# One encoder layer on one core: every product of x in Strassen blocks, the mixers in a stage of their own

## The chip, the cores and the metric

One core of a Trainium2 chip runs the whole layer. Its engines work side by side, each through its own queue in order: TensorE (PE, matrix products; its weight loads are listed as PEld), VectorE (DVE), ScalarE (ACT), GpSimd (POOL) and the DMA queues that SyncE (SP) issues. The metric is the device time of one execution in microseconds (us).

## The reference, cut to what matters

One layer with SEQ = 1024 rows and D_MODEL = 1024. x is multiplied by w_in (46 column tiles of 128) and by four gate matrices (32 column tiles). Four mixers of width 512 take parts of the first product.

```python
h = x @ w_in[l]
h_a, h_b, h_c, h_d = jnp.split(h, IN_SPLITS, axis=-1)
y_a = rglru_branch(...)        # convolution, two 64-wide gates, linear recurrence (scan), gelu
y_b = b_g * causal_dwconv(c_g * xh, sconv_w)
y_c = rwkv7_branch(h_c, ...)   # delta-rule recurrence over 1024 steps, 8 heads
y_d = chunk_attention(q, k, v, rel_bias)
merged = sum(sigmoid(x @ w_gate[n] + b_gate[n]) * (y[n] @ w_branch[n]) for n in range(4))
x = layer_norm(ALPHA * x + merged @ w_out, ...)
ff = square(relu(x @ w_ff1)) @ w_ff2
ple = (p @ w_ple) * sigmoid(x @ w_ple_gate + b_ple_gate)
x = layer_norm(ALPHA * x + ff + ple, ...)
```

## The kernel before, in words

Everything is kept transposed: a tile has 128 channels on the partitions and the 1024 rows along the free axis, in two halves of 512. A float32 product is made of three fast products: each operand is split into a high part (a copy by ACT, `Gemm.split` L347) and a low part (source minus high, by DVE, L348), and `Gemm.acc` (L367 to L369) adds high·high, high·low and low·high in a PSUM bank. With a depth of 1024, one column tile is 8 depth steps x 2 halves x 3 = 48 matmuls of 128x512.

The order of the program is as follows, with the times of the profile:

- 0 to 31 us: x comes in by eight 512 KB loads, and two column tiles (the low-rank inputs, C tiles 12 and 13) are accumulated in four banks as each slice of x lands.
- to about 115 us: six more C tiles (`zc_tile`) and `low_rank`, which makes decay, learning rate and gate of the RWKV mixer.
- about 115 to 977 us: the RWKV mixer, 16 units (two halves of the heads, eight stretches of 128 rows each). A unit inverts a triangular matrix in six levels; one level is a small product (`py` L246), an add on DVE (L247), a transpose on PE (`pt` L231) and a copy out on ACT (L232), each waiting for the one before. A unit runs at a raised priority (`HP`), and other work is put beside it: `run(oth, NO)` emits NO = 5 half column tiles of 24 matmuls (NOB = 6 in the first four units), held back by `issue_after` to behind the last inverse product of an earlier unit (L259, the unit's mark). That other work is the rest of the C tiles, q, k and v, then the recurrence `lru(j)` (L571 to L625) and the short convolution `sconv(j)` (L628 to L645) for j = 0 to 3, both reading their products straight from PSUM, and a few gate tiles.
- about 977 to 1040 us: three gate tiles, and loads of the finished branch outputs.
- 1040 to 1490 us: chunk attention, eight heads in 64 steps (`attend`), beside the branch products (`br`) and the remaining gate tiles (`ggt`).
- 1490 to 2413 us: w_out, layer norm, the seven-product feed-forward one (`seven`, L1054 on: a pair of weight tiles times x, as 2 x 2 blocks, takes 7 block products instead of 8, with sums of weight blocks on POOL and x blocks made on POOL and DVE beforehand), then feed-forward two and the last layer norm.

x stays split in 16 buffers throughout. A scheduler fixes the order of each engine's queue before the run; on the chip each queue is followed strictly in order, and an instruction at the head that waits holds what stands behind it.

Of the kernel before, what the change touches and what calls it, by code (L numbers as in the profile page):

```python
# [45 lines left out]
class Rwkv:  # L46
# [7 lines left out]
    PTAG = {"pt": "r", "py": "r", "p12": "r", "po": "o", "px": "s", "pss": "s", "pp": "s", "py2": "s"}  # L54
    BUFS = {t: 2 for t in ("ar", "bk", "bkT", "AA", "Qs", "TTf", "W", "SV", "bv", "D", "zt", "gn", "wm")}
    BUFS["gg"] = 3
    ALT = ("YT", "Y", "Yo")
# [30 lines left out]
    def unit(s, hf, b):  # L88
# [5 lines left out]
        def ps(n, w=512):  # L94
            tag = s.PTAG.get(n, "q")
            if tag == "r":
                tag += str(b % 2)
            return s.psum.tile([128, w], F32, tag=tag, name=n + u, bufs=PB[tag])

        def st(n, shape, tag=None, dt=F32):  # L100
            tag = tag or n
            if tag in s.ALT:
                tag += str(b % 2)
            return s.pool.tile(shape, dt, tag="rw_" + tag, name=n + u, bufs=s.BUFS.get(tag, 1))
# [150 lines left out]
        R = st("R", [128, 4, 128], dt=F32R)  # L255
# [9 lines left out]
        for c in range(2):  # L265
# [3 lines left out]
            PD = st("PD", [128, 2, 128])  # L269
# [51 lines left out]
HP = 3000  # L321
LAG = 2
NO = 5
NZ = 10
NB = 3
SK = 0
LO = 2
L0 = 3
N0 = 4
NOB = 6  # L330
DP = 2
PF = 4
NG = 14
NH = 8
NA = 1.6
# [37 lines left out]
def trunk(ctx, tc, xT, xn, pT, w_in, w_gate, w_branch, w_out, w_ff1, w_ff2, w_ple, w_pg,  # L373
# [6 lines left out]
    psum = ctx.enter_context(tc.tile_pool(name="psum", bufs=2, space=PSUM))  # L380
    bp = ctx.enter_context(tc.tile_pool(name="bp", bufs=1))
    tp = ctx.enter_context(tc.tile_pool(name="tp", bufs=4))
# [4 lines left out]

    def ps(tag, name, w=512):
        return psum.tile([128, w], F32, tag=tag, name=name, bufs=PB[tag])
# [3 lines left out]
    qkv = dr.tile([3, 4, 128, 1024], F32, name="qkv")  # L393
    gsd = dr.tile([32, 128, 1024], F32, name="gsd")
# [3 lines left out]
    xs = []  # L398

    def gemm_x(w, name, tag="g"):  # L400

        w = gm.load(w, 1024, name)
        for h in range(2):
            p = ps(tag, f"g{name}{h}")
            sl = slice(h * 512, h * 512 + 512)
            gm.acc(p, [w[k] + (xs[k][0][:, sl], xs[k][1][:, sl]) for k in range(8)])
            yield h, sl, p

    def gate(g):

        for h, sl, p in gemm_x(w_gate[g // 8, g % 8], f"gt{g}"):
            t = tmp(f"tg{g}{h}")
            A.activation(t, p, AF.Tanh, scale=0.5, bias=hbg[:, g:g + 1])  # L413
            yield h, sl, t

    def spill(g):
        for h, sl, t in gate(g):
            SY.dma_start(gsd[g, :, sl], t)
            yield 1

    spilled = [g for g in range(16) if g % 8 >= 1 + g // 8 * SK][:NG]


    with tc.tile_pool(name="mx", bufs=1) as mx:
        def t4(name, w=1024):
            return mx.tile([128, w], F32, tag="t4", name=name, bufs=6, padded_shape=[128, 1028])
# [7 lines left out]
        wt = [wp.tile([128, 1024], F32, tag="wf", name=f"wfc{i}", bufs=2) for i in (12, 13)]  # L434
        wf0 = [[], []]

        def first(i, c):
            wf, kw = wt[i][:, c:c + 512], [dict(name=f"w{t}c{12 + i}{c}") for t in "hl"]
            SY.dma_start(wf, w_in[W_C + 12 + i][:, c:c + 512])
            if i and c:  # L440
                wh, wl = (mx.tile([128, 512], F32R, tag=f"rw_{t}0", **k) for t, k in zip(("YT", "Y"), kw))
            else:
                wh, wl = (wp.tile([128, 512], F32R, tag=t, **k) for t, k in zip(("wh", "wl"), kw))
            gm.split(wf, wh, wl)
            wf0[i] += [(wh[:, k:k + 128], wl[:, k:k + 128]) for k in range(0, 512, 128)]

        zp = [[ps(t, f"gc{12 + i}{h}") for h in range(2)] for i, t in enumerate("gq")]
        first(0, 0)
        for k in range(8):
            xf = t4(f"xf{k}")  # L450
            SY.dma_start(xf, xT[k])
            xh = bp.tile([128, 1024], F32R, tag=f"s1_{k}", name=f"xh{k}")
            xl = bp.tile([128, 1024], F32R, tag=f"s2_{k}", name=f"xl{k}")
            gm.split(xf, xh, xl)
            xs.append((xh, xl))
            for i, c in {0: [(1, 0)], 1: [(0, 512)], 2: [(1, 512)]}.get(k, []):
                first(i, c)
            for i in range(2):
                for h in range(2):
                    sl = slice(h * 512, h * 512 + 512)  # L460
                    gm.acc(zp[i][h], [wf0[i][k] + (xh[:, sl], xl[:, sl])], k == 0, k == 7)
# [5 lines left out]
        V.tensor_scalar(hbg, hbg, 0.5, None, op0=ALU.mult)  # L467
        nh = cp.tile([128, 4], F32, name="nh")
        G.memset(nh, -0.5)

        cst = mx.tile([128, C_N], F32, name="cst")
        SY.dma_start(cst, cstd[:, 128:])
        pv = mx.tile([128, len(PV), 4], F32, name="pv")
        SY.dma_start(pv, pvd)
        mu = mx.tile([128, 2, 14], F32, name="mu")
        SY.dma_start(mu[:, 0, :], mud)
# [9 lines left out]
        def shifted(x, n, sl):  # L486
            return x[:, sl.start + n:sl.stop + n]
# [20 lines left out]
        def low_rank(d):  # L508


            def rw(tag, name, dt=F32R):
                return mx.tile([128, 512], dt, tag="rw_" + tag, name=name, bufs=R.BUFS[tag])
# [754 lines left out]
```

## Time and profile before

| | us |
|---|---|
| median of 3 runs | 2414.67 (2410.48 to 2416.7) |
| profiled execution, its own time | 2414.82 |
| span of the profiled execution | 2413.0 |
| PE busy | 2369.2 (98%), 12114 instructions |
| DVE busy | 1353.1 (56%) |
| ACT busy | 845.9 (35%) |
| POOL busy | 345.2 (14%) |
| mean granted TensorE clock | 0.990 of full speed |

Matmuls are pipelined, so the listed duration of one (about 395 ns) is longer than the distance between the starts of two, and a PE that counts as busy may still be switching or waiting between short instructions. The chain of waits gives 91% of the span to PE, 3% each to DVE and DMA.

### The profile page before, as it was taken

How to read it: one execution, taken by the hardware profiler on the slowest of the kernel's cores; microseconds unless marked ns; L12 is line 12 of the kernel's file. 1: busy time of each engine (PE TensorE's matmuls, PEld its weight loads, DVE VectorE, ACT ScalarE, POOL GpSimd, SP SyncE). 2: the span in 40 equal slices, each digit the busy share in tenths (PEclk: the TensorE clock that was granted, in tenths of full speed). 3: DMA queues.
4: the chain of work that ended last, by engine and by line, in shares of the span. 5: the costliest groups of instructions: out<-in, count | busy, mean ns of one | idle time of the engine just before them, and what ended most of it. 6: DMA issues, size and time to landing. Idle time of an engine off the chain costs nothing.

```text
span 2413.0 us, 31988 instructions
## 1 busy us (share of the span) xinstructions
PE 2369.2 (98%) x12114; PEld 1951.1 (81%) x12114; DVE 1353.1 (56%) x2758; ACT 845.9 (35%) x1478; POOL 345.2 (14%) x310
## 2 busy tenths in 40 slices
PE   9999999999999999999999999997999999999998
PEld 7888788777777778878888888876888888888886
DVE  5354545677677642245534334777644444776667
ACT  5543322424334222234434343334344444321110
POOL 0000100010000100000211100114145555000001
PEclk9999999999999999999999999998999999999999
DMA  5532222112121112254512224401123333532311
GB/s 200 192 126 70 88 71 70 56 53 66 53 71 53 64 60 77 98 174 125 158 53 73 80 76 142 164 31 57 44 96 111 112 114 130 187 123 89 103 53 70
DMA packets 123850, 231.33 MB, mean 96 GB/s; under 512 B 20016, under 2 KB 51888, under 8 KB 123696
## 3 DMA queue, kind: packets, MB, share of 16 engines
q1 hardware_dynamic: 123696, 229.29, 28.4%
q8 instruction: 95, 1.56, 0.3%
q14 instruction: 59, 0.48, 0.1%
HBM read 169.48 MB, written 59.77 MB: 95 GB/s over the span
## 4 chain that ended last, share of the span: by engine, by line
PE 91%; DVE 3%; DMA 3%; ACT 1%; issue 1%; POOL 0%; SPq 0%; DVEq 0%; ACTq 0%; POOLq 0%
PE f L368 5%; PE f L367 5%; PE f L369 5%; PE ggt L368 4%; PE ggt L369 4%; PE ggt L367 4%; PE af L369 2%; PE af L368 2%; PE af L367 2%; PE gc L368 2%; PE gc L369 2%; PE gc L367 2%; PE br L369 2%; PE br L367 2%; PE br L368 2%; PE gd L367 2%
## 5 line engine op out<-in xcount | busy, mean ns | idle before, releaser
L369 PE MATMUL ggt<-xh,wlgt 128*128 128x512 f32 x512 | 202.5, 396 | 0.0
L367 PE MATMUL ggt<-xh,whgt 128*128 128x512 f32 x512 | 202.4, 395 | 0.0
L368 PE MATMUL ggt<-xl,whgt 128*128 128x512 f32 x512 | 202.2, 395 | 0.0
L1183 DVE TENSOR_TENSOR x<-x,f 128x512 f32<-128x512 f32 x240 | 159.1, 684 | 74.1 <-PE f L369 73.4
L368 PE MATMUL f<-w2l,a2h 128*128 128x512 f32 x512 | 200.0, 391 | 0.0
L369 PE MATMUL f<-w2h,a2l 128*128 128x512 f32 x512 | 199.7, 390 | 0.0
L367 PE MATMUL f<-w2h,a2h 128*128 128x512 f32 x512 | 198.0, 390 | 0.0
L367 PEld LDWEIGHTS f<-w2h,a2h 128*128 128x128 f32 x512 | 96.0, 188 | 21.0 <-ACT w2h L347 0.3
L368 PEld LDWEIGHTS f<-w2l,a2h 128*128 128x128 f32 x512 | 96.1, 188 | 20.6
L369 PEld LDWEIGHTS f<-w2h,a2l 128*128 128x128 f32 x512 | 96.1, 188 | 20.6
L369 PEld LDWEIGHTS ggt<-xh,wlgt 128*128 128x128 f32 x512 | 96.2, 188 | 19.1 <-issue 0.5
L368 PEld LDWEIGHTS ggt<-xl,whgt 128*128 128x128 f32 x512 | 96.3, 188 | 19.0 <-issue 0.3
L367 PEld LDWEIGHTS ggt<-xh,whgt 128*128 128x128 f32 x512 | 96.3, 188 | 18.3
L367 PE MATMUL br<-yh,whwb 128*128 128x512 f32 x256 | 101.8, 398 | 3.2 <-ACT tg L413 1.8
L232 ACT ACTIVATE YT<-pt 128x512 fp32r<-128x512 f32 x96 | 56.8, 594 | 128.2 <-PE pt L231 126.0
L369 PE MATMUL br<-yh,wlwb 128*128 128x512 f32 x256 | 101.5, 396 | 0.1
L348 DVE TENSOR_TENSOR wlf<-wff,whf 128x512 fp32r<-128x512 f32 x80 | 65.7, 822 | 62.8 <-ACT whf L347 62.7
L368 PE MATMUL br<-yl,whwb 128*128 128x512 f32 x256 | 100.9, 394 | 0.0
L347 ACT ACTIVATE a2h<-a2f 128x1024 fp32r<-128x1024 f32 x32 | 34.0, 1061 | 177.9 <-PE f L368 109.4
L348 DVE TENSOR_TENSOR wlgt<-wfgt,whgt 128x512 fp32r<-128x512 f32 x64 | 46.8, 731 | 86.7 <-ACT whgt L347 84.5
L347 ACT ACTIVATE whf<-wff 128x512 fp32r<-128x512 f32 x80 | 50.6, 632 | 117.8 <-PE af L368 49.6
L369 PE MATMUL gc<-xh,wlc 128*128 128x512 f32 x224 | 88.1, 394 | 0.0
(490 smaller groups left out, 5962.6 us busy)
## 6 DMA issues: line engine op xcount, KB each, us to landing
wfgt<-w_gate SPq DMA_DIRECT2D x32, 512.0 KB, 3.3
wff<-w_ff SPq DMA_DIRECT2D x32, 512.0 KB, 3.3
a2f<-actd SPq DMA_DIRECT2D x32, 512.0 KB, 3.2
w2f<-w_ff SPq DMA_DIRECT2D x32, 512.0 KB, 3.9
gsd<-tg SPq DMA_DIRECT2D x44, 256.0 KB, 2.0
tl<-gsd SPq DMA_DIRECT2D x44, 256.0 KB, 3.1
zt<-zs SPq DMA_DIRECT2D x16, 640.0 KB, 4.9
qk<-qkv SPq DMA_DIRECT2D x64, 128.0 KB, 2.7
```

The lines of the kernel that those rows point to most:

```text
L232: A.activation(dst, heads(p), AF.Copy)
L347: s.nc.scalar.activation(hi, src, AF.Copy)
L348: s.nc.vector.tensor_tensor(lo, src, hi.bitcast(F32), op=ALU.subtract)
L367: mm(ps, lh, rh, start=first and i == 0, stop=False, **kw)
L368: mm(ps, lh, rl, start=False, stop=False, **kw)
L369: mm(ps, ll, rh, start=False, stop=last and i == n - 1, **kw)
L1183: V.tensor_tensor(x1[i][:, sl], x1[i][:, sl], p, op=ALU.add)
```

## The change

All 78 column tiles of x times w_in and w_gate are now made by `seven`, two tiles at a time: 39 pairs of 7 products, each product 4 depth steps x 3 = 12 matmuls. One pair takes 84 matmuls instead of 96. What else moves with it:

- x is kept as seven blocks (`XA`: 11, 21, T2, T1, T3, 22, T4, each split in four high and four low tiles), made at the start by `blocks()`: 4 subtractions on DVE, 12 on POOL, and 28 splits.
- Results come out in pieces at the end of several products. q, k, v go to DRAM unscaled (the 0.125 moves to the attention's loader), the 20 inputs of lru and sconv go to a new DRAM buffer `hd`, all 32 gates to `gsd`.
- To make room, RWKV's buffers are cut (single `YT`, `Y`, `Yo`, `AA`, `bk`, `TTf`; one PSUM bank `r0` for the inverse instead of two in turn). Beside a unit now stand NO = 11 products (NOB = 13 in the first four), 132 and 156 matmuls instead of 120 and 144.
- lru and sconv leave the RWKV stage. They run afterwards in a pool `my` of their own, with their inputs loaded from DRAM; sconv's two multiplications go to POOL. Four and eight of the remaining products stand between them in the program text.
- All gates are finished before the attention, x's pool is closed there, and the attention stands beside branch products only, in the order n = 2, 1, 0, with three steps (NA) per column tile.

```diff
-    PTAG = {"pt": "r", "py": "r", "p12": "r", "po": "o", "px": "s", "pss": "s", "pp": "s", "py2": "s"}
-    BUFS = {t: 2 for t in ("ar", "bk", "bkT", "AA", "Qs", "TTf", "W", "SV", "bv", "D", "zt", "gn", "wm")}
-    ALT = ("YT", "Y", "Yo")
+    PTAG = {"pt": "r0", "py": "r0", "p12": "r0", "po": "o", "px": "s", "pss": "s", "pp": "s", "py2": "s"}
+    BUFS = {t: 2 for t in ("ar", "bkT", "Qs", "W", "SV", "bv", "D", "gn", "gg")}
+    PB = {"r0": 1, "q": 2, "o": 1, "s": 1}
...
-NO = 5
-NOB = 6
-NA = 1.6
+NO = 11
+NOB = 13
+NA = 3
...
+    def seven(XB, w0, w1, name, done, tiles, bank, dst=None, load=None, sums=None):
...
+        a = bank("a", f"a{name}")
+        product(a11, 1, a, "11")
+        p1 = tiles(f"p1{name}")
+        A.activation(p1, a, AF.Copy)
+        yield 1
+        c = bank("c", f"c{name}")
+        product(a12, 2, c, "21")
+        result(0, 0, c, p1)
+        yield 1
+        s1 = total(1, a21, a22, ALU.add)
+        s2 = total(2, s1, a11, ALU.subtract)
+        product(s2, 3, a, "T2", first=False)
+        u2 = tiles(f"u2{name}")
+        A.activation(u2, a, AF.Copy)
...
+        product(s1, 4, b, "T1")
...
+        product(s3, 5, a, "T3", first=False)
...
+        product(s4, 6, b, "22", first=False)
...
+        product(a22, 7, a, "T4", first=False)
...
+        def blocks():
+            block("11", x11)
+            block("21", x21)
+            for k in range(4):
+                V.tensor_tensor(x11[k], x12[k], x11[k], op=ALU.subtract)
+            for k in range(4):
+                G.tensor_tensor(t2[k], x22[k], x11[k], op=ALU.subtract)
+            block("T2", t2)
+            block("T1", x11)
...
+        def others():
+            for i in (2, 6, 10):
+                yield from zc_pair(i)
+            for j in (0, 2):
+                for i in range(3):
+                    yield from qkv_pair(i, j)
+            for j in (0, 2):
+                for n in (0, 4, 12, 16, 8):
+                    yield from hd_pair(n + j)
+            for g in range(0, 32, 2):
+                yield from gate_pair(g)
...
-            for h, sl, p in gemm_x(w_in[W_A + j], f"xa{j}"):
-                A.activation(xa[:, 3 + h * 512:3 + h * 512 + 512], p, AF.Copy)
-                yield 1
+            SY.dma_start(xa[:, 3:1027], hd[j])
...
+            G.tensor_tensor(cx[:, 2:1026], cx[:, 2:1026], cc, op=ALU.mult)
...
-        oth = chain(zc(halves(1)), qkvs(), *(g for j in range(4) for g in (lru(j), sconv(j))), *(spill(g) for g in spilled[:NG - NB]))
+        for j in range(4):
+            sconv(j)
+            run(4)
+            lru(j)
+            run(8)
+        run(1000)
+    first.close()
...
-        for n in range(4):
+        attend(NA)
+        for n in (2, 1, 0, 3):
```

Three places in the queues follow, before and after. In the names, `lg` is a gate product of lru (the first digit after it is j), `gt` or `c` a product of a gate pair or C pair, `gya` a product of lru's second input; `py`, `pt`, `p12` with two numbers belong to the RWKV unit of that half and stretch.

The first is PE at the start. Before, the two first C tiles, 12 and 13, in four banks, where the second slice of x begins:

```order
L368 MATMUL gc130_101<-xl0_111,whc130_115 128x512
L368 MATMUL gc131_102<-xl0_111,whc130_115 128x512
L369 MATMUL gc130_101<-xh0_110,wlc130_116 128x512
L369 MATMUL gc131_102<-xh0_110,wlc130_116 128x512
L367 MATMUL gc120_99<-xh1_133,whc120_104 128x512
L367 MATMUL gc121_100<-xh1_133,whc120_104 128x512
L367 MATMUL gc130_101<-xh1_133,whc130_115 128x512
L367 MATMUL gc131_102<-xh1_133,whc130_115 128x512
```

Of the change, PE where the second product of pair c0 ends and the third product of pair c12 begins, and POOL's first sums up to the last part of the block T2 that this third product reads:

```order
L358 MATMUL cc0_276<-x21h3_245,whc02_277 128x512
L359 MATMUL cc0_276<-x21l3_246,whc02_277 128x512
L360 MATMUL cc0_276<-x21h3_245,wlc02_278 128x512
L358 MATMUL ac12_195<-xT2h0_314,whc123_334 128x512
L359 MATMUL ac12_195<-xT2l0_315,whc123_334 128x512
L360 MATMUL ac12_195<-xT2h0_314,wlc123_335 128x512
```

```order
L414 TENSOR_TENSOR S1c12_330<-wfA1_99 128x512
L414 TENSOR_TENSOR S2c12_332<-S1c12_330,wfA0_98 128x512
L443 TENSOR_TENSOR wfA1_99<-wfA0_98,wfA1_99 128x512
L533 TENSOR_TENSOR xT20_306<-xf220_128,xf000_101 128x512
L539 TENSOR_TENSOR xf010_120<-xf220_128,xf010_120 128x512
L533 TENSOR_TENSOR xT21_308<-xf221_130,xf001_103 128x512
L539 TENSOR_TENSOR xf011_122<-xf221_130,xf011_122 128x512
L533 TENSOR_TENSOR xT22_310<-xf222_132,xf002_105 128x512
L539 TENSOR_TENSOR xf012_124<-xf222_132,xf012_124 128x512
L543 TENSOR_TENSOR xf100_110<-xf100_110,xT20_306 128x512
L533 TENSOR_TENSOR xT23_312<-xf223_134,xf003_107 128x512
```

The first slice of x with two tiles of weights was all that PE needed for each step before; now its queue goes on to block T2, whose four parts are made by POOL behind and among other sums.

The second is PE at the end of RWKV unit 3 of the second half. Before:

```order
L596 MATMUL lg310_7047<-xc3_7030,wri3_6964 128x512
L231 MATMUL pt_1_3_6358<-ident_267,Y_1_3_6266 128x128 x4
L246 MATMUL py_1_4_6735<-Yo_1_4_6733,YT_1_4_6726 128x64 x4
L596 MATMUL lg311_7050<-xc3_7030,wri3_6964 128x512
L151 MATMUL pn_1_5_7126<-cst_274,sq_1_5_7124 128x2 x2
L231 MATMUL pt_1_4_6742<-ident_267,Y_1_4_6711 128x128 x4
L252 MATMUL py_1_3_6364<-idr_290 128x512
L254 MATMUL py_1_3_6364<-Y_1_3_6266,AA_1_3_6222 128x128 x4
L182 MATMUL pbg_1_5_7155<-rk_1_5_7152,cst_274 128x256
L259 MATMUL p12_1_3_6372<-YT_1_3_6357,R_1_3_6370 128x128 x4
L367 MATMUL gya31_7386<-xh0_110,whya30_7072 128x512
```

Of the change, the same unit:

```order
L360 MATMUL bgt4_7889<-xT1h3_386,wlgt44_7891 128x512
L227 MATMUL pt_1_3_7058<-ident_144,Y_1_3_6997 128x128 x4
L242 MATMUL py_1_3_7066<-Yo_1_3_7064,YT_1_3_7057 128x64 x4
L227 MATMUL pt_1_3_7073<-ident_144,Y_1_3_6997 128x128 x4
L242 MATMUL py_1_3_7082<-Yo_1_3_7079,YT_1_3_7072 128x64 x4
L227 MATMUL pt_1_3_7089<-ident_144,Y_1_3_6997 128x128 x4
L248 MATMUL py_1_3_7095<-idr_169 128x512
L250 MATMUL py_1_3_7095<-Y_1_3_6997,AA_1_3_6953 128x128 x4
L255 MATMUL p12_1_3_7103<-YT_1_3_7088,R_1_3_7101 128x128 x4
L358 MATMUL agt4_7828<-xT3h0_432,whgt45_8190 128x512
```

Before, the next unit's chain (unit 4 of the second half) and the lru products stand between the levels; now the levels follow one another with nothing between.

The third is PE at lru's products for j = 1. Before, in the middle of the RWKV stage:

```order
L246 MATMUL py_1_0_4846<-Yo_1_0_4844,YT_1_0_4835 128x64 x4
L219 MATMUL pw_1_0_4824<-SV_1_0_4818,AA_1_0_4793 64x64 x7
L596 MATMUL lg100_5167<-xc1_5156,wri1_5090 128x512
L246 MATMUL py_0_7_4474<-Yo_0_7_4471,YT_0_7_4464 128x64 x4
L231 MATMUL pt_1_0_4853<-ident_267,Y_1_0_4837 128x128 x4
L596 MATMUL lg101_5170<-xc1_5156,wri1_5090 128x512
L596 MATMUL lg110_5173<-xc1_5156,wri1_5090 128x512
L231 MATMUL pt_0_7_4481<-ident_267,Y_0_7_4389 128x128 x4
L246 MATMUL py_1_0_4861<-Yo_1_0_4859,YT_1_0_4852 128x64 x4
L596 MATMUL lg111_5176<-xc1_5156,wri1_5090 128x512
L151 MATMUL pn_1_1_5252<-cst_274,sq_1_1_5250 128x2 x2
```

Of the change, after the last product of the last gate pair, with all three last j's and then the attention's scores (`p20`):

```order
L359 MATMUL agt30_10873<-xT4l3_568,whgt307_10993 128x512
L360 MATMUL agt30_10873<-xT4h3_567,wlgt307_10994 128x512
L755 MATMUL lg100_9897<-xc1_9886,wri1_9881 128x512
L755 MATMUL lg101_9900<-xc1_9886,wri1_9881 128x512
L755 MATMUL lg110_9903<-xc1_9886,wri1_9881 128x512
L755 MATMUL lg111_9906<-xc1_9886,wri1_9881 128x512
...
L755 MATMUL lg211_10228<-xc2_10208,wri2_10203 128x512
L755 MATMUL lg300_10539<-xc3_10528,wri3_10523 128x512
...
L755 MATMUL lg311_10548<-xc3_10528,wri3_10523 128x512
L871 MATMUL p20_0_0_11082<-kh0_11037,q20_11036 128x128
```

On DVE the same stretch holds 17 instructions of j = 0 and then all of j = 1, 2, 3, with no split of a gate weight among them; before, the same 32 per j, and four multiplications, stand among those of RWKV units and weight splits.

## Rows read from the trace of the kernel before

**Rows 1.** The page: share of the chain of waits by engine.

```profile
PE 91%; DVE 3%; DMA 3%; ACT 1%; issue 1%; POOL 0%; SPq 0%; DVEq 0%; ACTq 0%; POOLq 0%
```

**Rows 2.** Busy time by stretch: start:end, length, PE, PEld, DVE, ACT, POOL (instructions), clock, DMA share, GB/s.

```profile
0.00:31.00 31.00, 28.45 (x116) 20.77 (x117) 20.73 (x55) 17.91 (x27) 1.91 (x15) 1.00 0.74 269
...
500.00:600.00 100.00, 98.59 (x588) 79.03 (x587) 72.00 (x164) 37.90 (x66) 10.03 (x15) 1.00 0.19 60
...
1750.00:2050.00 300.00, 300.00 (x1330) 248.38 (x1329) 137.16 (x169) 128.28 (x218) 158.07 (x121) 1.00 0.32 113
```

**Rows 3.** The chain of waits in order of time: start, length, what.

```profile
9.59 0.91 PE gc L367 x4
...
453.31 0.86 PE lg L596 x2
...
537.56 1.09 PE pq L195 x8
...
889.02 1.08 PE pq L195 x8
```

**Rows 4.** The timeline of DVE: two levels of one unit's inverse (start, length).

```profile
293.10 0.40 DVE L247 TENSOR_TENSOR Y<-Y,py 128x256 fp32r<-128x256 f32 x1
...
295.88 0.41 DVE L247 TENSOR_TENSOR Y<-Y,py 128x256 fp32r<-128x256 f32 x1
```

**Rows 5.** Busy time by stretch, columns as in rows 2, around one bare inverse.

```profile
295.00:301.00 6.00, 3.60 (x25) 3.01 (x25) 3.43 (x11) 2.11 (x5) 0.00 (x0) 1.00 0.39 113
301.00:308.00 7.00, 6.91 (x25) 5.86 (x24) 2.23 (x4) 0.00 (x0) 0.00 (x0) 0.52 0.01 1
```

**Rows 6.** DVE by line, 440 to 880 us: busy, mean ns, idle before, releaser.

```profile
L642 DVE SCALAR_TENSOR_TENSOR cv<-cx,pv,cv 128x512 f32<-128x512 f32 x16 | 13.8, 863 | 0.2
L590 DVE SCALAR_TENSOR_TENSOR xc<-xa,pv,xc 128x512 f32<-128x512 f32 x18 | 13.4, 746 | 0.3
...
L599 DVE SCALAR_TENSOR_TENSOR ti<-ti,xc 128x512 f32<-128x512 f32 x8 | 5.5, 687 | 7.1 <-ACT ti L597 7.1
...
L610 DVE SCALAR_TENSOR_TENSOR ti<-ti,m 128x512 f32<-128x512 f32 x8 | 5.2, 689 | 5.8 <-ACT m L608 5.8
L623 DVE SCALAR_TENSOR_TENSOR y<-y,ya 128x512 f32<-128x512 f32 x8 | 5.2, 688 | 6.9 <-ACT y L621 6.9
...
L611 DVE TENSOR_TENSOR_SCAN m<-aa,m,ti 128x512 f32<-128x512 f32 x4 | 5.1, 1276 | 0.0
...
L611 DVE TENSOR_TENSOR_SCAN m<-aa,ti 128x512 f32<-128x512 f32 x4 | 4.9, 1218 | 0.0
...
L640 DVE TENSOR_SCALAR cv<-cx,pv 128x512 f32<-128x512 f32 x8 | 3.9, 483 | 0.1
...
L619 DVE TENSOR_SCALAR y<-y 128x512 f32<-128x512 f32 x8 | 3.0, 415 | 0.0
```

**Rows 7.** The chain of waits, columns as in rows 3, where the attention stage begins.

```profile
1018.90 2.11 DMA ys<-y
1025.01 5.73 DMA yf<-ys
...
1041.95 3.44 DMA qk<-qkv
```

**Rows 8.** POOL by line, columns as in rows 6.

```profile
L1097 POOL TENSOR_TENSOR wff<-wff,wff 128x512 f32<-128x512 f32 x16 | 21.3, 1328 | 0.0
...
L1037 POOL TENSOR_TENSOR x1R<-x1R,x1R 128x512 f32<-128x512 f32 x4 | 14.0, 3531 | 4.6 <-DVE x1R L1026 4.6
```

**Rows 9.** ACT by line in the attention, 1040 to 1490 us, columns as in rows 6.

```profile
L771 ACT ACTIVATE S<-S,sm 128x640 f32<-128x640 f32 x32 | 26.4, 826 | 12.1 <-DVE sm L767 11.0 <-DVE sm L769 0.9
...
L783 ACT ACTIVATE PT<-pt 128x512 f32<-128x512 f32 x40 | 23.5, 589 | 25.3 <-PE pt L782 25.2
...
L771 ACT ACTIVATION_READ_ACCUMULATOR S<-S,sm 128x1 f32 x64 | 12.1, 188 | 0.0
...
L783 ACT ACTIVATE PT<-pt 128x128 f32<-128x128 f32 x40 | 10.8, 271 | 24.9 <-PE pt L782 24.9
```

More of the change, by code (lines that the diff above doesn't have):

```diff
@@ L447, in trunk @@
[L447 to L461, printed above, removed]
+        early = [f"rw_{t}" for t in ("ar", "ar", "Qs", "Qs", "bkT", "bkT", "SV", "SV", "AA", "bk", "bh", "wm", "YT", "Y", "TTf", "zt")]
@@ new lines, in spare, with xraw, part @@
+        def spare(name):
+            t = early.pop(0)
+            return mx.tile([128, 512], F32, tag=t, name=name, bufs=Rwkv.BUFS.get(t[3:], 1))
+        def xraw(kb, j, name, make=spare):
+            r = []
+            for k in range(4):
+                t = make(f"xf{kb}{j}{k}") if make is spare else make(k)
+                SY.dma_start(t, xT[4 * kb + k][:, j * 512:j * 512 + 512])
+                r.append(t)
+            return r
+        def part(name, k, which, dt=F32R, tile_name=None):
+            return xp.tile([128, 512], dt, tag=f"x{name}{which}{k}", name=tile_name or f"x{name}{which}{k}")
@@ new lines, in block, with wraw @@
+        def block(name, src):
+            for k in range(4):
+                hi, lo = part(name, k, "h"), part(name, k, "l")
+                gm.split(src[k], hi, lo)
+                XA[name, k] = (hi, lo)
+        def wraw(w, tiles):
+            for h, t in enumerate(tiles):
+                SY.dma_start(t, w[:, h * 512:h * 512 + 512])
+        wA = [wp.tile([128, 1024], F32, tag="wf", name=f"wfA{i}", bufs=2) for i in range(2)]
+        halves_of = lambda t: (t[:, 0:512], t[:, 512:1024])
+        wraw(w_in[W_C + 12][:, 0:512], [wA[0][:, 0:512]])
@@ new lines, in trunk, with bank_b @@
+        V.tensor_scalar(hb, pv[:, 0:2, :], 0.5, None, op0=ALU.mult)
+        R.setup(mx)
+        def bank_b(which, name):
+            return ps({"a": "q", "b": "q", "c": "o"}[which], name)
+        gb = blocks()
+        ga = [zc_pair(12, load=[h for t in wA for h in halves_of(t)]), zc_pair(0, load=wB, sums=tmp, bank=bank_b)]
+        for _ in range(7):
+            next(gb)
+            for g in ga:
+                next(g)
+        for g in (*ga, zc_pair(4)):
+            for _ in g:
+                pass
@@ new lines, in run @@
+        def run(n):
+            for _ in range(n):
+                if next(oth, None) is None:
+                    return
+        marks = []
+        for hf in range(2):
+            R.start_half(hf)
+            for b in range(8):
+                with tc.high_priority(HP):
+                    marks.append(R.unit(hf, b))
+                with ExitStack() as after:
+                    if len(marks) > max(LAG, L0):
+                        after.enter_context(tc.issue_after(marks[-1 - LAG]))
+                    run(NO if len(marks) > N0 else NOB)
```

393 lines of the change are left out of this document (173 added, 220 removed).

## The prediction

> **What bounds the kernel now.** I read the chain of waits first: nine tenths of it is PE [rows 1]. Then the busy time by stretch: the stretches with long products are full, and in the RWKV stage PE still counts as 98% busy while DVE stands at 72% [rows 2]. So fewer matmuls shorten the kernel, as long as PE's queue stays fed. The price of a 128x512 product comes from the chain: four take 0.91 us, 0.2275 us each [rows 3]; 1330 in 300 us is 0.2256 us with a few records missing [rows 2]. The listed 395 ns is a pipelined duration and may not be used.
>
> PE's busy share hides small waits. In the RWKV stage the units follow each other every 50.2 us: from the score products at 537.56 to those at 889.02 there are seven units [rows 3]. The 120 products beside a unit are 120 x 0.2275 = 27.3 us of it; the other 22.9 are its own small products and the waits inside its inverse. A level of the inverse, from one add on DVE to the next of the same unit, takes 295.88 - 293.10 = 2.8 us [rows 4]. In 6 us of such levels, two units in turn, PE was busy for 3.60 [rows 5], so a level holds about 0.9 us of PE work and 1.9 of waiting where nothing stands between. Of the 22.9 us I put 5 to 7 down to waiting, about three bare levels' worth (an estimate).
>
> The queues are followed in order, so the places where the change leaves PE's queue with nothing but a waiting chain are read from the order, and priced from these rows.
>
> **The change part by part.**
>
> *Fewer products.* 78 tiles x 48 = 3744 matmuls become 39 x 84 = 3276: 468 x 0.2275 = **-106 us**, all on PE's path. The other products stay. More sums come with it (four results per pair on DVE and ACT, four weight sums on POOL), all under 12 matmuls of 2.7 us per product: per product some 1.4 us of DVE (a split and a result, each of L599's size, 0.69 [rows 6]) and two passes of ACT like L783's 0.59 [rows 9], so they hide. The feed-forward stage already runs this pattern without a wait: 300 us out of 300 [rows 2].
>
> *Start.* Before, PE works from 6 us on: 28.45 us of the first 31 count as busy and 116 matmuls are 26.4 us of pure work [rows 2], 4.6 us lost. Now 48 matmuls (11 us) of blocks 11 and 21 can run first, and half of them need the weights of pair c0, which land after 5.5 MB; at 269 GB/s [rows 2] that is 20 us. Then PE's queue stands at block T2. Its last part is the 11th sum on POOL, and eight of these follow the last slice of x (after 5 MB, 19 us, or earlier with a faster start). A POOL sum takes 1.33 us in the feed-forward and 3.53 us beside dense DVE work [rows 8]: 8 sums are 11 or 28 us, so T2 is ready at 28 to 46 us, and PE has lost 17 to 35 us instead of 4.6. Later blocks follow within the work of the others. I take **+20 us**, nearer the quick price since DVE has pauses here, and keep 8 to 45. The Trainium skill says beside this (GPSIMD Engine Reference, section 1, Specifications) that POOL shares its SBUF interfaces with VectorE and contends with instructions of two SBUF inputs. The splits and subtractions here are of that kind; by that rule alone the slow row would hold and the term would be near its upper end.
>
> *RWKV units.* A unit now has 132 products beside it, so the stage takes its share of work earlier; that is in the count above. What is new is where they stand: with single buffers and one bank the next unit's chain no longer runs between the levels, and the order shows the last two to three levels and the products up to the mark with nothing between. Three bare levels wait 3 x (2.8 - 0.9) = 5.7 us, and the step from the last product over DVE to the mark about 2; that is 7.7 us against 5 to 7 now, so about 1 us x 16 = **+18 us** with a little for the first units, whose products run out early. Bounds: if the twelve more products all lie in today's waits, 12 x 0.2275 = 2.7 us per unit are won, -44; if a unit waits 4 us more, +60.
>
> *Mixers.* This is the largest cost. In PE's queue the lru products of j = 1, 2, 3 stand one behind the other after the last product of the last gate pair, and the attention's scores behind them. PE can only wait while DVE works through j = 1, 2 and 3 and the end of j = 0. Per j DVE has 32 instructions [rows 6]: 6 x 0.746 (xc), 4 x 0.863 (cv), 4 like L640 at 0.48 (the first steps of both), 12 like L599, L610 and L623 at 0.69, 4 like L619 at 0.42, and the scans 1.218 + 1.276. That is 22.3 us. To this come its waits for ACT, which four j's show as 7.1 + 5.8 + 6.9 us [rows 6], 5.0 per j: 27.3 us. Three of them are 82 us; the end of j = 0, 17 instructions of 24 single steps, is 13 more beyond the last gate products. Then the attention's first loads: SP's queue issues them behind the store of the last lru output, and such a step takes 2.11 us for the store and 3.44 for the load [rows 7], with split and issue about 10 us. The lru products themselves, 12 of 0.86 / 2 us [rows 3], some 6 us with their switches, are in the count of before. 82 + 13 + 10 - 6 = **+98 us**. None of it lies under PE work, since no product is left behind the last gate pair but those that need these outputs. Lower bound 70 (DVE steps shorten when nothing runs beside, and the j's overlap better); upper 120 (loads of 3 to 6 us [rows 7] and POOL's two multiplications in each j's chain). What was hidden under RWKV before costs nothing there now: DVE's 22.3 x 4 us at 72% of a stage that PE bounds gave nothing back.
>
> *Attention.* In its first half the branch products stand between the steps. In the second (pairs 2 and 3) some 30 of the 64 steps have 33 products among them, so PE waits for ACT: exponential 0.83 + 0.19 us and two copies 0.59 + 0.27 [rows 9], 1.88 us per step, and PE's own products are about as long. A step waits 0 to 2 us; I take 0.6, **+18 us** (0 to 60). The gate products that stood there before are in the count.
>
> The remaining edits (q's 0.125, the copy of block (1,0) by ACT, `hd` through DRAM with 10 MB each way at a DMA share of about 0.2 [rows 2]) hide under PE.
>
> Sum, against the profiled execution: 2413.0 us span and 1.8 around it make 2414.8, and the median of the runs is 2414.67, the same. 2414.8 - 106 + 20 + 18 + 98 + 18 = **2462 us**.
>
> **The rivals.**
>
> *The waits of the units take in the products* (faster). The place is the RWKV stage, the price 2.7 us per unit. If the chain of a unit, not PE, sets the pitch of 50 us, twelve more products per unit cost nothing: -44 instead of +18, and the sum is 2400. It decides from the point where this term is below -30, since 20 + 98 + 18 = 136 must fall under 106. For it: 5 to 7 us of waiting per unit. Against it: the order puts the products ahead of the bare levels, not between them. Chance 0.14.
>
> *The clock falls after the bare chains.* At 295 to 301 us PE waited much, and in the next 7 us the granted clock was 0.52, the lower of its two levels, 1.2 GHz [rows 5]. At half speed these 7 us cost 3.4. If each of 16 units ends in that way, 16 x 3.4 = 54 us come on top, and some 7 in the attention: 2523. Against it: before, it happened after two units of 16 only. The Trainium skill (TensorE: Matmul & The Clock Gate, HAM oscillation — how this bites in real kernels) says that a wait between bursts makes each next burst start at the low clock, for every such wait. That speaks for this rival; the trace agrees in 2 units of 16. Chance 0.12.
>
> *The single chain sets the pitch.* With one YT, one Y and one bank, a unit's inverse cannot begin before the last has ended. Six levels of 2.8 us, the steps around them and the 132 products would then add rather than overlap: 50.2 us become 52.9 by PE's count and about 58 with the waits, 16 x 4.9 = 78 us instead of 18: 2522. Chance 0.08.
>
> **How the numbers follow.** The forecast case has 0.66. Its terms vary by about 30 us together, 2410 to 2520. About 0.3%, 7 us, is what a measurement can tell from no change. Of the forecast's 0.66, 0.03 end below 2407 and 0.05 within 7 us; of the first rival's 0.14, 0.09 are faster and 0.03 the same. Faster 0.12, same 0.08, slower 0.80. The range 2398 to 2530 holds most of the forecast, half of the first rival and most of the other two.
>
> **What would show it.** In the profile after: PE busy near 2265 us of work in a longer span; a stretch of some 95 us behind the last gate product with PE nearly idle, DVE near 80% and short lru products in it; the first 45 us with PE at half or less and POOL busy; units about 54 us apart. It would be wrong if DVE had done j = 1 and 2 before the last gate product, or if the units came every 50 us in spite of 132 products.

## The result and the profile after

The change is slower: 2651.81 us (2646.14 to 2658.53) against 2412.57 us (2409.93 to 2416.7) of the kernel before, a ratio of 1.0991 with a 95% interval of 1.0955 to 1.1027. Slower was forecast, but 2651.81 us lies 122 us above the upper end of the range.

The page of the profile after: busy time, then PE and the granted clock in 40 slices of 66 us (tenths).

```profile
PE 2394.6 (90%) x11646; PEld 1948.0 (73%) x11646; DVE 1574.7 (59%) x2984; ACT 976.6 (37%) x1745; POOL 610.0 (23%) x503
...
PE   5999899998899999999319998799799999999998
...
PEclk7999798988889898999659998699899999999999
```

The clock line of the page before, for comparison:

```profile
PEclk9999999999999999999999999998999999999999
```

A 9 stands for 90% or more. PE has its 468 instructions less, 11646 instead of 12114, and yet more busy time than before (2394.6 against 2369.2 us): the mean granted clock was 0.916 instead of 0.990. The digits show four bad places: the start; the RWKV stage up to slice 16, where the clock is often at 8 instead of 9; a hole in the middle (PE 3 and 1, clock 6 and 5); and the end of the attention (clock 8 and 6 in slices 25 and 26).

Busy time of the kernel after by stretch (start:end, length, PE, PEld, DVE, ACT, POOL with counts, clock, DMA share, GB/s), two stretches of which answer to [rows 2]:

```profile
0.00:31.00 31.00, 10.73 (x26) 4.67 (x26) 23.35 (x23) 14.61 (x25) 19.34 (x26) 0.71 0.66 222
500.00:600.00 100.00, 93.30 (x525) 74.33 (x523) 58.65 (x135) 32.13 (x65) 21.34 (x23) 0.93 0.25 81
...
1285.00:1395.00 110.00, 18.84 (x24) 7.03 (x24) 72.75 (x113) 39.26 (x42) 19.23 (x5) 0.56 0.33 114
```

In the first 31 us PE made 26 matmuls instead of 116; in 500 to 600 us it made 525 instead of 588; for 110 us behind the last gate product it made 24.

To see where the time went I cut both traces at four events: the first and the last RWKV mark, the first attention score, the first product of w_out. In each stage the 128x512 products of the split kind (high and low parts) are counted, and a stage's loss is the change of its length plus 0.2275 us [rows 3] for each product that it has less. So, by the way they are made, the losses minus 468 x 0.2275 = 106.5 us are the whole difference. The 32 recorded lru products, which move from the RWKV stage to the mixers, are not counted; with them the two losses would be 121 and 120 us.

| stage | before: us / products | after: us / products | loss, us | forecast |
|---|---|---|---|---|
| start to the first mark | 225.3 / 826 | 262.8 / 828 | 37 | 20 (8 to 45) |
| first to last mark (RWKV) | 751.9 / 1880 | 933.7 / 2179 | 114 | 18 (-44 to 60) |
| last mark to the first score (mixers) | 57.0 / 225 | 199.3 / 293 | 127 | 98 (70 to 120) |
| attention to w_out | 480.2 / 1557 | 356.1 / 708 | 69 | 18 (0 to 60) |
| the rest | 898.6 / 3744 | 902.1 / 3756 | 1 | 0 |

The sum is 347 - 106 = +241 us, the difference of the two spans (2653.9 and 2413.0). That a product is worth 0.2275 us in the kernel after too is read from its feed-forward: 1326 products in the 300 us from 2000 to 2300, against 1330 in 300 us before [rows 2]. The same ledger is used for every experiment below.

### The profile page after: what moved, and what is told of

Read it like the earlier page. It is cut to its first block, busy times and chain, and to the rows that moved or that the text cites. A ratio compares the mean times of both kernels' runs of the same rounds, so it can differ in the third digit from the quotient of the medians.

```text
span 2653.9 us, 32488 instructions
## 1 busy us (share of the span) xinstructions
PE 2394.6 (90%) x11646; PEld 1948.0 (73%) x11646; DVE 1574.7 (59%) x2984; ACT 976.6 (37%) x1745; POOL 610.0 (23%) x503
## 5 line engine op out<-in xcount | busy, mean ns | idle before, releaser
L1042 POOL TENSOR_TENSOR mvn<-mvn,nh 128x1 f32<-128x1 f32 x16 | 15.0, 937 | 408.7 <-DVE mvn L1041 406.0
L338 ACT ACTIVATE whgt<-wfgt 128x512 fp32r<-128x512 f32 x80 | 50.4, 630 | 139.9 <-PE agt L359 47.5
L1005 POOL TENSOR_TENSOR acc<-acc,tl 128x512 f32<-128x512 f32 x32 | 45.1, 1411 | 202.9 <-DVE tl L1003 200.0
L227 PE MATMUL pt<-ident,Y 128*128 128x128 f32 x384 | 68.6, 307 | 18.8 <-DVE Y L243 18.7
L755 PE MATMUL lg<-xc,wri 128*128 128x512 f32 x32 | 22.8, 866 | 69.3 <-issue 69.3
L242 PEld LDWEIGHTS py<-Yo,YT 128*128 128x128 f32 x384 | 58.6, 210 | 35.9 <-ACT YT L228 29.0
L242 PE MATMUL py<-Yo,YT 128*128 128x64 f32 x384 | 63.6, 291 | 21.9 <-ACT YT L228 16.5
L339 DVE TENSOR_TENSOR wlgt<-wfgt,whgt 128x512 fp32r<-128x512 f32 x80 | 65.8, 823 | 27.2 <-ACT whgt L338 25.7
```

What stands on the lines that cost most here:

```text
L227: T.transpose(p[:, h * 128:h * 128 + 128], src.bitcast(F32)[:, h, :], ident)
L242: T.matmul(p1[:, h * 64:(h + 1) * 64], YT[:, h, :], Yo[:, h * 64:(h + 1) * 64], start=True, stop=True)
L338: s.nc.scalar.activation(hi, src, AF.Copy)
L339: s.nc.vector.tensor_tensor(lo, src, hi.bitcast(F32), op=ALU.subtract)
L755: T.matmul(p, wri[:, t, :], xc[:, h * 512:h * 512 + 512], start=True, stop=True)
L1005: G.tensor_tensor(acc[jp, h][:, jo, :], acc[jp, h][:, jo, :], gt[h], op=ALU.add)
```

## The experiments

**RWKV: which part of the change costs 114 us?** e1 puts only the cut buffers into the kernel before.

```diff
-    PTAG = {"pt": "r", "py": "r", "p12": "r", ...
-    BUFS = {t: 2 for t in ("ar", "bk", "bkT", "AA", "Qs", "TTf", "W", "SV", "bv", "D", "zt", "gn", "wm")}
-    BUFS["gg"] = 3
-    ALT = ("YT", "Y", "Yo")
+    PTAG = {"pt": "r0", "py": "r0", "p12": "r0", ...
+    BUFS = {t: 2 for t in ("ar", "bkT", "Qs", "W", "SV", "bv", "D", "gn", "gg")}
+    ALT = ()
...
-        R = st("R", [128, 4, 128], dt=F32R)
+        R = st("R", [128, 4, 128], "bh", F32R)
```

> The kernel before with only the RWKV buffers of the change: single YT, Y, Yo, AA, bk, TTf and others, one PSUM bank for the inverse, R and PD in shared buffers; products, NO, mixers and attention as before. Theory A (the single chain is what made the units of the change 59.6 us long instead of 49.5): units come every 56 to 60 us, the total rises by 90 to 140 us to 2505 to 2550 us, and the granted clock in the stage falls to about 0.9. Rival B (the length comes from the seven-product work beside the units, from how much of it there is and where its results go): units stay within 2 us of 50, total within 25 us of before.

Measured: 2585.75 us, ratio 1.0724 (1.0687 to 1.076). But for the first and the last two, the units come every 53 to 67 us; the RWKV stage loses 147 us, the clock in 400 to 1000 us lies between 0.81 and 0.94. Theory A holds, and by more than it gave: without any change to the products, the buffers alone cost 174 us.

e4 tries the reverse, with YT, Y, Yo and the PSUM bank doubled in the change.

> The change with YT, Y and Yo and the inverse's PSUM bank doubled again, alternating from unit to unit. Room for it is made with 2 instead of 3 PSUM banks for the products and 5 instead of 8 of the 512-wide buffers. Theory A (the single chain costs the RWKV stage): units come every 52 to 55 us, total 2550 to 2600 us. Rival B (it is the products' place in the queue, or the products themselves): units stay at 58 us or more, total 2630 us or more.

Measured: 2639.88 us (1.0948, 1.0916 to 1.098), middle units still 59 to 63 us apart, RWKV loss 119. By the letter rival B. But the order of that kernel still shows bare levels, since AA is read by the last product of a unit and R lies in the buffer that the next unit's front writes. So theory A was put more sharply: any one buffer that lives through the whole inverse keeps the next unit back. e5 and e6 test two groups of them, each alone, in the kernel before: AA and R, and YT, Y, Yo with the PSUM bank. e7 undoes both groups in the change (bk, TTf and some others stay single).

```diff
# e5
-    BUFS = {t: 2 for t in ("ar", "bk", "bkT", "AA", "Qs", ...
+    BUFS = {t: 2 for t in ("ar", "bk", "bkT", "Qs", ...
-        R = st("R", [128, 4, 128], dt=F32R)
+        R = st("R", [128, 4, 128], "bh", F32R)
# e6
-    PTAG = {"pt": "r", "py": "r", "p12": "r", ...
-    ALT = ("YT", "Y", "Yo")
+    PTAG = {"pt": "r0", "py": "r0", "p12": "r0", ...
+    ALT = ()
```

> The kernel before with two of the change's cuts only: AA in a single buffer, and R (the last product's input) in the buffer of bh. AA is read by the last product of a unit's inverse and written at the front of the next unit's, so this alone should keep two inverses from running side by side. Theory A1 (any one buffer that spans the whole inverse is enough to lay the units end to end): 110 to 175 us slower, 2520 to 2590 us, units of 55 to 61 us. Rival B1 (YT, Y, Yo and the PSUM bank are what matters): within 30 us of before.

> The kernel before with only YT, Y, Yo and the inverse's PSUM bank single; AA, bk, TTf and the others stay double. Theory A1: this alone lays the inverses end to end too, though the next unit's scores and front can still be made beside the levels: 60 to 150 us slower, 2470 to 2560 us. Rival B1' (AA is the only one that counts): within 30 us of before.

Measured: e5 2560.65 us (1.0612, 1.0581 to 1.0642), e6 2554.32 us (1.0585, 1.0555 to 1.0616); RWKV losses 130 and 122 us. Each group alone costs nearly what all the cuts together cost (147). They don't add up, so undoing one group gives next to nothing back (e4). Single buffers within a group were not tested.

> The change with YT, Y, Yo, AA doubled, R in a buffer of its own and two PSUM banks for the inverse; room from two banks for the products, 5 instead of 8 of the 512-wide buffers, 3 instead of 4 of the C results and a single W. Theory A1 (doubling YT, Y and Yo alone did nothing because AA and R still held the next unit back): units of 52 to 55 us, the granted clock in that stage back above 0.95, total 2510 to 2550 us. Rival C (the products beside the units are themselves in the way, by their place in the queue or by two banks): units stay at 57 us or more, total above 2590 us.

Measured: 2522.6 us (1.0454, 1.0424 to 1.0484), 129 us less than the change. The RWKV loss fell from 114 to 5 us, with units 39 to 64 us apart in turns, 52 on average, and the mixers' loss from 127 to 98. Theory A1 is shown: it was the buffers, not the products beside the units, which are the change's own in e7.

e9 asks how much of it is the clock. It adds to e1 products that nobody reads, in the waits of the last four levels.

```diff
+        def warm(src, n):
+            for _ in range(n):
+                T.matmul(heads(dm), src[:, 0, :], s.idr[:, None, :].to_broadcast((128, 4, 128)), start=True, stop=True)
...
+            if li >= 2:
+                warm(YT, 2)
...
+            if li >= 2:
+                warm(Y, 3)
```

> The kernel of e1 (before, with the change's single RWKV buffers) and 23 products per unit that nobody reads, into the PSUM bank that is free there: two behind each small product and three behind each transpose of the last four levels of an inverse, where PE otherwise waits. They add no work to any chain but some 0.7 to 1.4 us per unit where they stand ahead of a level. It separates the low clock from the bare waiting. Theory K (a good part of the RWKV loss is the low clock: small products at half speed in the bare levels and some ten products at half speed behind them): granted clock in the stage back to 0.97 or more, small products as short as before, total 25 to 60 us below e1, 2525 to 2560 us. Rival W (only the waiting for DVE and ACT counts, the clock costs little): total within 15 us of e1 or slower by the 23 x 0.2275 x 16 = 84 us of added products.

Measured: 2553.48 us (1.0588, 1.0559 to 1.0617), 32 us less than e1 although 368 products were added. The timeline of a unit's end, first in the kernel after (start, length, engine, line, what; in brackets the wait before):

```profile
538.28 0.69 PE L227 MATMUL pt<-ident,Y 128*128 128x128 f32 x4 [0.51 <-DVE Y L243]
...
539.72 1.06 PE L242 MATMUL py<-Yo,YT 128*128 128x64 f32 x4 [0.75 <-DVE Y L239]
540.82 0.42 DVE L243 TENSOR_TENSOR Y<-Y,py 128x256 fp32r<-128x256 f32 x1 [1.11 <-PE py L242]
...
541.29 1.11 PE L227 MATMUL pt<-ident,Y 128*128 128x128 f32 x4 [0.52 <-DVE Y L243]
...
543.75 1.91 PE L250 MATMUL py<-Y,AA 128*128 128x128 f32 x8
```

and in e9, where the same steps have other line numbers:

```profile
726.26 0.63 PE L251 MATMUL py<-Yo,YT 128*128 128x64 f32 x4
...
727.53 0.66 PE L230 MATMUL pt<-ident,Y 128*128 128x128 f32 x4
...
729.65 1.06 PE L263 MATMUL py<-Y,AA 128*128 128x128 f32 x8
```

Within one bare tail `pt` goes from 0.69 to 1.11 us; kept busy, the same steps stay at 0.63, 0.66 and 1.06. The clock of one 100 us stretch, e1 and then e9:

```profile
700.00:800.00 100.00, 90.51 (x465) 71.37 (x465) 60.28 (x142) 32.74 (x55) 8.53 (x12) 0.86 0.17 54
```

```profile
700.00:800.00 100.00, 94.83 (x526) 74.09 (x525) 63.84 (x143) 33.09 (x57) 9.24 (x10) 0.98 0.15 48
```

So theory K holds at its lower end: at least 32 us of e1's 174 are the low clock. e9 still loses 124 us in the RWKV stage at a clock of 0.98; how much of that is plain waiting and how much the added products (at most 84 us) is not told apart. The rule of the Trainium skill that was weighed ahead (TensorE: Matmul & The Clock Gate, HAM oscillation — how this bites in real kernels), that waits between bursts bring the low clock each time, agrees here: in the kernel after it came behind each of the first 14 units, it held 0.86 in that stretch of e1, and it was all but gone when the waits were filled (0.98).

**Mixers.** e3 leaves more products for their stage.

```diff
-NO = 11
+NO = 8
```

> The change with NO = 8 instead of 11: 96 products beside a unit instead of 132, so 36 more products (97 us of PE) are left for the stage of the mixers. Theory A (the mixers' gap of about 115 us is for want of products, and a unit's waits do not depend on how many stand beside it): units shorten by 8 us each to about 52, the gap shrinks to 20 to 50 us, total 2565 to 2600 us. Rival B (the unit's chain sets the pitch, so fewer products do not shorten it): units stay near 59 us, the gap shrinks all the same, and the total is 2640 to 2680 us.

Measured: 2610.84 us (1.0828, 1.0796 to 1.0859): 11 us above theory A's range. The mixers' loss fell from 127 to 81 us, but the middle units came every 51 to 56 us, 6 us shorter instead of 8, and the RWKV loss rose to 126. With the buffers undone, e8 does it again.

> The same with NO = 8, so that 36 products of 2.7 us go from the units to the mixers' stage. Theory A1 with the mixers' gap as a want of products: the units shorten by the products they lose (to 45 to 48 us) and the gap by 60 to 80 us, total 2440 to 2480 us. Rival D (an inverse has a length of its own near 50 us, so lighter units do not end earlier): units stay at 50 us or more, total 2490 to 2530 us.

Measured: 2465.28 us (1.0216, 1.0187 to 1.0246), 57 us less than e7. Middle units 44 us apart on average, RWKV loss 0, mixers' loss from 98 to 59. e10 prices lru itself: in the change, lru's second input is copied through for j = 2 and 3.

```diff
-            lru(j)
+            if j < 2:
+                lru(j)
+            else:
+                y2 = t4(f"y2{j}")
+                SY.dma_start(y2, hd[4 + j])
+                SY.dma_start(ysd[0][j], y2)
```

> The change without the recurrence for j = 2 and 3: their second input is copied through to the branch buffer instead, so 2 x 26 DVE instructions, 8 short products and their ACT work are left out. Theory M (the gap behind the last gate product is DVE's work for j = 1 to 3 in order, PE waits for all of it): the total falls by the lru share of two j's, 2 x 18 to 24 us, 2604 to 2618 us. Rival N (the gap is held by loads from DRAM or by POOL's multiplications in the convolution): at most 15 us less.

Measured: 2598.5 us (1.0775, 1.0744 to 1.0806): 53 us less than the change, more than theory M's 36 to 48. In the mixers' stage it is 46, 23 per j, inside that range; the attention, whose code is the same, lost 14 us less (see there). PE's timeline of the kernel after, from the last product of the last gate pair:

```profile
1276.99 0.39 PE L360 MATMUL agt<-xT4h,wlgt 128*128 128x512 f32 x1
1299.23 5.72 PE L755 MATMUL lg<-xc,wri 128*128 128x512 f32 x8 [21.85 <-issue]
1328.28 6.56 PE L755 MATMUL lg<-xc,wri 128*128 128x512 f32 x8 [23.32 <-issue]
1358.99 6.56 PE L755 MATMUL lg<-xc,wri 128*128 128x512 f32 x8 [24.16 <-issue]
1395.79 0.77 PE L871 MATMUL p<-kh,q 128*128 128x128 f32 x2 [30.24 <-ACT kh L338]
```

The waits of the kernel after, PE and then DVE, 1270 to 1396 us (engine, line, releaser: us in total, times, longest):

```profile
PE lg L755 <- issue: 69.3, 3, 24.2
PE p L871 <- ACT kh L338: 30.2, 1, 30.2
```

```profile
DVE ti L758 <- ACT ti L756: 21.8, 7, 5.7
...
DVE ti L769 <- ACT m L767: 5.4, 4, 1.6
DVE m L765 <- ACT m L763: 5.3, 4, 1.4
```

PE waited three times, once for each j, up to 24.2 us, and once 30.2 us from the last lru product to the first score. Between the lru products of one j and the next lie 29 and 31 us: DVE's steps, and its waits for ACT. Theory M holds, with the ACT steps in the chain: DVE was busy for 73 of the 110 us.

**Attention.** e2 makes all gates ahead of the attention in the kernel before, with their results held in the mixers' pool so that it can't begin earlier.

```diff
-    spilled = [g for g in range(16) if g % 8 >= 1 + g // 8 * SK][:NG]
+    spilled = list(range(32))
-NB = 3
-NG = 14
-NH = 8
-NA = 1.6
+NB = 0
+NG = 32
+NH = 0
+NA = 3
...
-            SY.dma_start(gsd[g, :, sl], t)
+            t = t4(f"tg{g}{h}", 512)
```

> The kernel before with all 32 gate tiles made before the attention begins (their results are held in a buffer of the mixers' pool, which closes first), and three attention steps asked for per branch tile as in the change; products, RWKV and mixers as before. It prices the attention beside branch products only. Theory A (the second half of the attention runs dry of products): 45 to 75 us slower than before, 2460 to 2490 us, with PE at 60 to 80% busy for some 100 us near the attention's end. Rival B (the loss there comes from the order n = 2, 1, 0 or from x's pool being closed): at most 15 us slower.

Measured: 2485.65 us (1.0308, 1.0279 to 1.0338), +74 us, 56 of them in the attention and 15 ahead of it. Theory A holds, in the sum and in its sign: PE was busy for 40.83 of the 50 us from 1450 and 33.39 of the next 50. e12 asks whether spreading the branch products over all steps wins that back.

```diff
+                    with ExitStack() as after:
+                        if n != 3 and len(steps) > LAGA:
+                            after.enter_context(tc.issue_after(steps[-1 - LAGA]))
+                        gm.acc(p, [wb[k] + (ysp[k][0][:, sl], ysp[k][1][:, sl]) for k in range(4)])
```

> The kernel of e11 with the branch products beside the attention held back: each may only follow the last product of the attention step two before the latest one asked for, so that they are spread over all 64 steps instead of running out half way. Theory R (the attention's loss is that its second half has no products): 25 to 45 us off the 58 us that the attention stage still loses, total 2408 to 2430 us against 2453 of e11. Rival S (branch products are too few whatever their place, 708 against the 1557 of before, or the heads' loads set the pace): at most 12 us less, 2441 to 2455 us.

Measured: 2484.5 us (1.0302, 1.0276 to 1.0329) against 2453.3 of e11, whose kernel it changes: 31 us slower, outside the ranges of both theories. From the first score to the last value product it took 318 us, in e11 316, and what had been held back stood over behind it (56 us from there to w_out instead of 26).

The ledger, cut at the middle of the 480 value products, says why. The change loses 16 us in the first half and 50 in the second, where it has 34 products instead of 577. e11 loses 21 and 31, e12 44 and 31. So the dry half is where most of the change's loss lies, but 155 more products there cost e12 their whole time, and the first half, with 249 fewer, lost 23 us more. Theory R falls as a remedy: on this reading the products are too few for all the steps, wherever they stand. The clock was lower in e12 too, and its share of the 31 us is not told apart.

Part of the loss goes with the clock. The attention of the change and of e10 is the same code, with the same 1717 instructions on PE; e10 (and e3 likewise) lost 55 us there instead of 69. The attention stage of the change, then of e10:

```profile
1395.80:1751.90 356.10, 323.11 (x1717) 279.14 (x1718) 189.38 (x575) 147.08 (x325) 45.09 (x32) 0.87 0.38 118
```

```profile
1354.70:1696.40 341.70, 308.32 (x1717) 265.42 (x1718) 190.72 (x576) 148.36 (x325) 45.46 (x32) 0.93 0.38 123
```

Before, the clock of this stage was 1.00; in e11 it was 0.92, in e12 0.88. The chain of waits of e11 there:

```profile
1232.15 3.11 DMA qk<-qkv
...
1237.23 3.00 DMA qk<-qkv
...
1242.19 2.73 DMA qk<-qkv
...
1246.88 2.77 DMA qk<-qkv
```

Every 5 us a load, the next one only when the one before has been split: there is one buffer for them. e14 gives two, e15 also two for the transposed v.

```diff
-            return ap.tile([128, 512], F32, tag="qk", name=name, bufs=1)
+            return ap.tile([128, 512], F32, tag="qk", name=name, bufs=2)
```

> The kernel of e11 with two buffers instead of one for the loads of q, k and v (128x512 each), so that one half loads while the other is split. Theory V (with few products beside it the attention is set by the chain of single-buffered loads, four per head of 2.8 us and the split behind each): the attention stage loses 15 to 35 us of its 55, total 2420 to 2440 us against 2453 of e11. Rival X (the steps' own work on PE, ACT and DVE sets it): within 6 us of e11.

> The same with two buffers for the transposed v too, so that the next pair's v need not wait for the last values of the pair before. Theory V: another 5 to 12 us less than e14, three changes of pair of 2 to 4 us each. Rival X: within 4 us of e14.

Measured: e14 2439.28 us (1.0122, 1.0105 to 1.0139), 14 us less than e11, with the attention stage at 324 instead of 342 us and its loss at 37 instead of 55. e15 2443.1 us (1.0118, 1.0082 to 1.0153), no gain over e14. So a second buffer for the loads takes away 18 of e11's 55 us; the second v buffer gives nothing. The clock rose with it, from 0.92 to 0.96, and how much of the 18 us is the clock no run tells. What the other 37 us are, the steps' own work, their waits for each other or the clock, no run here tells apart.

**Start.** e11 moves the 12 sums of x blocks to DVE, in the kernel of e8.

```diff
-                G.tensor_tensor(t2[k], x22[k], x11[k], op=ALU.subtract)
+                V.tensor_tensor(t2[k], x22[k], x11[k], op=ALU.subtract)
```

> The kernel of e8 with the 12 sums of x blocks on DVE instead of POOL. In the trace of the change POOL's sums and DVE's splits went in turns from 14 to 47 us, 1.7 us each, against 0.69 for a split alone. Theory P (POOL's sums slow DVE by more than they spare it): the start is 10 to 18 us shorter, total 2445 to 2456 us against 2465 of e8. Rival Q (DVE is the bound at the start, and 12 x 0.69 us more make it longer): 0 to 10 us longer, 2465 to 2475 us.

Measured: 2453.3 us (1.0183, 1.0156 to 1.021), 12 us less than e8; the start's loss fell from 42 to 35 us, and another 5 us came off in the RWKV stage. The timeline of the kernel after, POOL and DVE, shows how the sums cost DVE time:

```profile
17.96 1.71 POOL L533 TENSOR_TENSOR xT<-xf,xf 128x512 f32<-128x512 f32 x1
18.46 1.75 DVE L529 TENSOR_TENSOR xf<-xf,xf 128x512 f32<-128x512 f32 x1
19.62 1.71 POOL L539 TENSOR_TENSOR xf<-xf,xf 128x512 f32<-128x512 f32 x1
20.13 1.75 DVE L339 TENSOR_TENSOR xT1l<-xf,xT1h 128x512 fp32r<-128x512 f32 x1
```

and e11's, DVE:

```profile
19.41 0.69 DVE L534 TENSOR_TENSOR xf<-xf,xf 128x512 f32<-128x512 f32 x1
20.01 0.69 DVE L344 TENSOR_TENSOR xT1l<-xf,xT1h 128x512 fp32r<-128x512 f32 x1
20.61 0.69 DVE L534 TENSOR_TENSOR xf<-xf,xf 128x512 f32<-128x512 f32 x1
21.21 0.69 DVE L538 TENSOR_TENSOR xT<-xf,xf 128x512 f32<-128x512 f32 x1
```

The two engines went in turns, one instruction of each every 1.67 us: a DVE instruction of 0.69 us took 1.75 beside a POOL sum. Theory P holds for the total; the start itself became 6 us shorter, not 10 to 18. So the sums are not the whole start. PE's longest wait there, and the ACT step that stood ahead of what it waited for, in the kernel after:

```profile
25.82 0.80 PE L358 MATMUL ac<-x11h,whc 128*128 128x512 f32 x1 [15.10 <-ACT whc L338]
```

```profile
23.58 0.63 ACT L338 ACTIVATE xT1h<-xf 128x512 fp32r<-128x512 f32 x1 [2.71 <-DVE xf L529]
```

PE waited for the high part of the weights of pair c0. They had landed by 21.3 us, but in ACT's queue their split stands behind those of the block T1, and these wait for DVE's subtractions (L529). In e11 this wait was still 11.9 us. What an order with the weights' split first would give was not run.

**What is left.** e13 is e12 with NO = 6.

> The kernel of e12 with NO = 6: 24 more products, 65 us of PE, go from the RWKV units to the mixers' stage. Theory T (the mixers' stage still wants products): its loss falls from 59 to 25 to 40 us and the units lose nothing, total 20 to 35 us below e12. Rival U (the mixers' stage is bound by DVE, whose share there is 85%, and each product brings 1.4 us of DVE work; or the units wait more with 72 products beside them): within 12 us of e12, or slower.

Measured: 2483.3 us (1.0289, 1.0262 to 1.0317), the same as e12. The mixers' loss went from 62 to 56 us only, and the units lost 12 us. Theory T falls, and rival U's time holds. DVE was busy 158 of 200 us there, so it is not full; what holds the mixers' last 56 to 60 us is open. No version beat the kernel before. The best, e14, is 1.2% slower: 35 us lost at the start, 61 in the mixers, 37 in the attention, against 106 won.

## Why the prediction was right and wrong

- *Fewer products, -106*: right. The trace has the 468 products less, and the feed-forward, at 1326 products in 300 us, went at the pace of before.
- *Start, +20*: 37, inside the bounds of 8 to 45, but at another place. I had PE stand at block T2; there it waited 1.8 and 1.3 us. It stood 15.1 us, and later 7.1, for the high part of weights that ACT split late. I took the quick POOL price "since DVE has pauses here". From 14 us on DVE had hardly any: POOL's sums took 1.71 us and stretched DVE's. The rule of the Trainium skill named there (GPSIMD Engine Reference, section 1, Specifications) agrees with the trace in that the two engines slowed each other; the slow row of 3.53 us, which I had tied to it, did not come.
- *RWKV units, +18*: the step that failed, 114 us measured. The places were right, bare levels at each unit's end. The size was wrong in two ways. I set the bare levels against "5 to 7" us of waiting that a unit had already and took the difference, about 1 us. But before, two chains ran side by side and each covered the other; with single buffers the whole inverse lay on the path, and e1, e5 and e6 show 122 to 147 us for that. And I took the clock as a rival for itself and the single chain as another, with 2523 and 2522 us, when the bare chain is what brings the clock down: e9 gives at least 32 us of it. The two came together, at a joint chance that I had not given.
- *Mixers, +98* (its terms, 82 + 13 + 10 - 6, make 99): 127, above the bound of 120; with the lru products counted, as I had counted them, 120. The reading was right: PE waited for the three j's one after the other. From the last gate product to the first score it took 118 us where I had 105. A j took 29 to 31 us instead of 27.3. And the lru products, for which I took 6 us off, held PE for 19 us at a clock of 0.56; I had also priced 12 of them at 0.43 us, when each stands in the trace as two, 0.86 us together [rows 3].
- *Attention, +18*: 69, above the bound of 60. The place was right, 50 us of it in the second half. The size was wrong: I gave 30 steps without products 0.6 us of wait each, and the loss there comes to 1.7 us for each of them (an estimate, 50 / 30). I had left out two things. The loads of q, k and v go through a single buffer, in the kernel before too, where 1557 products covered them; a second one took away 18 of e11's 55 us (e14). And the clock fell, for which I had 7 us in a rival; the same code at 0.93 instead of 0.87 lost 14 us less (e10).
- *First rival* (the units take in the products, -44): it came in no kernel. With both groups of buffers undone the products beside a unit cost their time, no less: the RWKV loss was 5 us in e7 and -7 at best (e12). The forecast of slower held because every loss had the same sign; four of four terms were set too small.

## What to carry to other kernels

Before cutting buffers to make room, list those that live from the front of a serial chain to its end: here either of two groups of them, held single, laid neighbouring chains end to end, and undoing only one of the two gave next to nothing back. When work moves away from a stage, ask what its own length is without that cover (chains, loads through one buffer), since a cover hides waits that the profile of before doesn't list. And price a bare chain with the low clock in it, not beside it as a separate case.

## What the runs showed of the hardware that was not expected

- DVE and POOL, both with two inputs from SBUF, went in turns: from 16 to 36 us one instruction of each every 1.67 us, listed at 1.75 and 1.71 us, where DVE alone takes 0.69 (e11).
- Adding 368 products that nobody reads made a kernel 32 us faster, since the granted clock stayed at 0.97 to 1.00 in three stretches of 100 us (e9) instead of 0.81 to 0.94 in six (e1).
- The same attention code, with the same instructions on PE, took 356 us at a granted clock of 0.87 and 342 us at 0.93 (the kernel after and e10).
